# Stick-breaking attention in a decoder layer: the subtraction that makes log beta moved from VectorE to GpSimd

## The chip, the cores and the metric

The kernel runs on one core of a Trainium2 chip. The core has five engines that work side by side: TensorE (PE in the profile; its weight loads are PEld), VectorE (DVE), ScalarE (ACT), GpSimd (POOL) and SyncE (SP), which issues most DMAs. Each engine takes its instructions strictly from its own queue; semaphores order them against the other engines. The metric is the device time of one execution in microseconds.

## The reference

One inference step of a decoder layer, for a prompt of 1024 tokens and 8 sample sequences of 8 tokens with 512 cached ones. The layer is a SwiGLU half step, a mixer (attention, a state-space branch, two gates) and a second SwiGLU half step. What matters here is the attention:

```
z = einsum('bqhd,bkhd->bhqk', q, k) * 64 ** -0.5 + bias
mask = k_pos[None, :] < q_pos[:, None]
log_beta = log_sigmoid(z)
log_keep = where(mask, log_beta - z, 0.0)
after = cumsum(log_keep, axis=3, reverse=True) - log_keep
w = where(mask, exp(log_beta + after), 0.0)
out = einsum('bhqk,bkhd->bqhd', w, v)
```

With e = log(1 + exp(z)), log_beta is z - e and log_keep is -e. A weight is therefore exp(z - e - sum of e over the later keys).

## The kernel before

All matrix products are made in parts: an f32 operand is split into an f16 high part and an f16 rest, so a product takes several f16 matmuls. The stages follow each other: first SwiGLU, the mixer's projections and state-space branch (`mixer_a`, first half), the attention stage (`mixer_a`, second half), the branches' sum (`mixer_b`), second SwiGLU.

In the attention stage `attend_prompt` goes over 4 pairs of heads, 2 chunks of 512 queries and blocks of 128 keys, from the last key block of a chunk down to the first: 4 blocks in the first chunk and 8 in the second, 48 in all. The blocks on the diagonal have 128, 256, 384 and 512 queries, all others 512. A block holds both heads of the pair side by side, so a full block is 128 partitions by 1024 columns; the profile names the smaller ones 256, 512 and 768.

`weights_of` makes one block. TensorE writes the logits into PSUM (L1091, mask L1096); ScalarE makes |z| into tile `ae` (L1098), and z is made into tile `az`, one head by ScalarE (L1100) and one by VectorE (L1102). ScalarE does the exponential and the logarithm in `ae` (L1016, L1017), VectorE adds max(z, 0) (L1018): `ae` now holds e. L1019 makes z - e in place in `az`. ScalarE rounds e, scaled, to f16 (L1021, tile `ah`: the high part), and VectorE makes the rest (L1025), which it writes as f16 into the very tile `ae` from which it reads e:

Of the kernel before, what the change touches and what calls it, by code (L numbers as in the profile page):

```python
# [1004 lines left out]
def weights_of(k, n, hh, rk, acc, logits, after, w=None, first=True, c=(1.0, -1.0)):  # L1005

    nc = k.nc
    v = nc.vector  # L1010
    az = k.ring.tile([P, 2, 512], F32, tag="r", bufs=6, name="az")
    ae = k.ring.tile([P, 2, 512], F32, tag="r", bufs=6, name="ae")
    ah = k.ring.tile([P, 2, 512], F16, tag="h", bufs=4, name="ah")
    z, e = az[:rk, :hh, :n], ae[:rk, :hh, :n]
    logits(az, ae)
    nc.scalar.activation(e, e, AF.Exp, scale=-1.0)  # L1016
    nc.scalar.activation(e, e, AF.Ln, bias=1.0)  # L1017
    v.scalar_tensor_tensor(e, z, 0.0, e, op0=ALU.max, op1=ALU.add)  # L1018
    v.tensor_sub(z, z, e)  # L1019
    hi = ah[:rk, :hh, :n]  # L1020
    nc.scalar.activation(hi, e, AF.Copy, scale=c[0])  # L1021
    if hh == 1:
        after(e)
    lo = ae.bitcast(F16).rearrange("p h (n two) -> p h two n", two=2)[:rk, :hh, 0, :n]
    v.scalar_tensor_tensor(lo, e, c[0], hi, op0=ALU.mult, op1=ALU.subtract)  # L1025
    for h in range(hh):
        for j, part in enumerate((hi, lo)):
            nc.tensor.matmul(acc[:rk, h, :], k.tri[:rk, :rk], part[:, h, :], start=first and j == 0, stop=True,
                             skip_group_check=True)
    v.scalar_tensor_tensor(z, acc[:rk], c[1], z, op0=ALU.mult, op1=ALU.add)  # L1030
    w = z if w is None else w[:rk].unsqueeze(1)
    nc.scalar.activation(w, z, AF.Exp)
    if hh == 2 and after:
        after(hi, lo)
    return w
# [37 lines left out]
def attend_prompt(k, qT, kT, vt, pairs, scales):  # L1073

    nc = k.nc
    for p in pairs:
        qs, ks, inv, c = scales[p]
        for qc in range(2):
# [3 lines left out]
            for j in range(top, -1, -1):  # L1082
# [21 lines left out]
                def rest(hi, lo):  # L1104
                    for h in range(2):
                        for part in (hi, lo):
                            nc.tensor.matmul(acc[:, h, q0:], k.earlier, part[:, h, :], start=False, stop=True,
                                             skip_group_check=True)

                w = weights_of(k, n, 2, P, acc[:, :, q0:], logits, rest if j else None, None, j == top, c)  # L1110
                for h in range(2):
                    nc.tensor.matmul(po[64 * h:64 * h + 64, q0:], vt[:, j, (2 * p + h) * DH:(2 * p + h + 1) * DH],  # L1112
# [11 lines left out]
def attend_sample(k, dr, qT, kT, vt):  # L1124
# [56 lines left out]
    kps = pages("cache_k", NPG - 1)  # L1181
    acc = k.psz.tile([P, 1, 512], F32, tag="z")
    weights_of(k, 512, 1, NS, acc, new_logits, keep_sum(NS, True), w)
    wh = heads(w)
    po = z_tile([P, NB, H // 2, 2, LS])
# [7 lines left out]
    for pg in range(NPG - 1, -1, -1):  # L1193
# [15 lines left out]
        acc = k.psz.tile([P, 1, 512], F32, tag="z")  # L1209
        nc.tensor.matmul(acc[:, 0, :], k.ones, e_sum[:, 0, :], start=True, stop=True, skip_group_check=True)  # L1210
        weights_of(k, 512, 1, P, acc, logits, keep_sum(P, False), w, False)
        vps = pages("cache_v", pg)
        yield
# [628 lines left out]
```

TensorE multiplies both parts with the triangle `tri` (L1028) into the accumulator `P` in PSUM, which gives the sum over the later keys of the block; VectorE combines it with z - e (L1030), ScalarE takes the exponential (L1032), TensorE multiplies with v (L1112). The matmuls with `earlier` (L1107) complete the accumulator for the next block once L1030 has read it. The accumulator has one buffer, the logits' PSUM tiles two, `az` and `ae` share six buffers, `ah` has four.

Three other things share the stage. `attend_sample` attends for the sample tokens, a step after each fourth block: it fetches cache pages by indirect DMAs on GpSimd's queue (L1144, 64 of them in groups of eight; a group takes the four tiles of the group before), multiplies with them (L1155), and uses `weights_of` with hh == 1, five times. The gate projections (`project`, matmuls of L226 with 364 or 360 columns) are placed between the blocks as filler for TensorE until they run out. Their weights are loaded, measured (VectorE's L89 for the maximum of a partition, GpSimd's PARTITION_ALL_REDUCE at L82 across partitions) and split (L101, L102). `scaled_pair` reduces the maxima of the next pair's q and k the same way (GpSimd at L1048).

The order on each engine isn't the order of the code: a scheduler sets it when the program is built, from its own estimate of durations. So an instruction that moves to another engine can change the order on all of them.

## Time and profile before

| | us |
|---|---|
| median of 3 runs | 2384.77 |
| lowest, highest run | 2381.21, 2393.02 |
| the profiled execution's own time | 2397.24 |
| its span, first to last instruction | 2395.5 |
| granted TensorE clock, mean share | 0.982 |

The attention stage reaches from about 1118 to 1490 us of the span. The profile comes from one execution. The page gives the busy time of each engine over the whole span; views by stretch give it for parts. A row of the view in order of time has a start, a duration, the engine, the line, the operation and, in brackets, the idle time of the engine before it and what ended it; "issue" there means that no semaphore of the profile ended it.

### The profile page before, as it was taken

To read this page: it belongs to the slowest core of one execution; us is meant where nothing else is said; L and a number is where in the kernel's file an instruction comes from. 1 tells how busy PE (TensorE), PEld (TensorE's weight loads), DVE (VectorE), ACT (ScalarE), POOL (GpSimd) and SP (SyncE) were. 2 spreads that over 40 slices of the span, in tenths; PEclk is the share of its full clock that TensorE was granted. 3 is DMA by queue.
4 is the path that set the end of the run, shared out by engine and by line. 5 is a ranking of instruction groups with operands and counts; after the bars stand their busy time and mean duration, and the time that the engine had idled before them with its cause. 6 is when DMAs were issued, how large, how long until landed. Compare 5 with 4: busy or idle time off the path is not lost.

```text
span 2395.5 us, 42875 instructions
## 1 busy us (share of the span) xinstructions
PE 2287.6 (95%) x18391; PEld 1626.9 (68%) x18391; DVE 1678.2 (70%) x3026; ACT 969.2 (40%) x1244; POOL 141.8 (6%) x193
## 2 busy tenths in 40 slices
PE   5999999999999999899999997999999999999997
PEld 2677778777787666685544452655688878888884
DVE  5966698886797626446788787697677655777735
ACT  3533331233331521245788787324443321333403
POOL 0000000000000000001133300000000000000000
PEclk8999999999999999989999998999999999999999
DMA  8133334433333144445244323522111143111302
GB/s 308 55 119 108 108 120 140 152 108 123 135 145 126 54 146 146 110 158 185 75 137 136 109 67 128 187 77 84 61 52 55 34 139 111 63 54 54 129 19 76
DMA packets 94191, 262.83 MB, mean 110 GB/s; under 512 B 13152, under 2 KB 50400, under 8 KB 83760
## 3 DMA queue, kind: packets, MB, share of 16 engines
q1 hardware_dynamic: 83632, 240.23, 29.3%
q0 software_dynamic: 5312, 17.34, 2.5%
q10 hardware_dynamic: 5056, 2.52, 0.5%
q8 instruction: 144, 2.36, 0.4%
q14 instruction: 47, 0.39, 0.1%
HBM read 204.10 MB, written 49.66 MB: 106 GB/s over the span
## 4 chain that ended last, share of the span: by engine, by line
PE 54%; DVE 13%; ACT 7%; DMA 5%; issue 3%; POOL 1%; SPq 1%; another core or an unknown queue 0%; ACTq 0%; DVEq 0%; POOLq 0%
PE u L481 19%; PE u L242 13%; PE u L226 11%; PE u L216 2%; PE z L1368 2%; DVE wl L102 2%; DVE mx L89 2%; DMA wf<-in_ffn_w_in 2%; ACT ae L1098 1%; DMA wf<-in_w_in 1%; PE z L226 1%; PE z L994 1%; PE o L1112 1%; DMA aw<-in_ada_w 1%; ACT ae L1016 1%
## 5 line engine op out<-in xcount | busy, mean ns | idle before, releaser
L226 PE MATMUL u<-u,wh 128*128 128x364 f16 (+1 forms) x1632 | 391.6, 319 | 6.3 <-ACT u L398 4.3
L242 PE MATMUL u<-h,wh 128*128 128x272 f16 (+1 forms) x2304 | 366.2, 280 | 4.9 <-DVE h L102 4.9
L101 ACT ACTIVATE wh<-wf,sc 128x1024 f16<-128x1024 f32 (+2 forms) x130 | 183.2, 1410 | 371.4 <-PE u L242 179.8
L89 DVE TENSOR_REDUCE mx<-wf 128x1 f32<-128x1024 f32 (+2 forms) x136 | 211.1, 1575 | 145.3 <-DMA wf<-in_ffn_w_in 80.3
L481 PE MATMUL u<-u,wh 128*128 128x272 f16 (+1 forms) x1824 | 288.0, 279 | 1.7 <-DVE mx L89 1.3
L242 PEld LDWEIGHTS <-wh 128*128 128x128 f16 x2560 | 249.2, 97 | 59.3 <-issue 6.9
L481 PEld LDWEIGHTS <-wh 128*128 128x128 f16 x2432 | 234.6, 98 | 66.3 <-issue 19.7
L226 PE MATMUL u<-u,wl 128*128 128x364 f16 (+1 forms) x816 | 260.2, 319 | 1.1 <-DVE wl L102 1.1
L102 DVE SCALAR_TENSOR_TENSOR wl<-wf,sc,wh 128x1024 f16<-128x1024 f32 (+2 forms) x130 | 209.2, 1609 | 73.3 <-ACT wh L101 72.8
L226 PEld LDWEIGHTS <-wh 128*128 128x128 f16 x1824 | 176.4, 98 | 114.7 <-issue 15.0
L242 PE MATMUL u<-h,wl 128*128 128x274 f16 (+1 forms) x1152 | 228.3, 280 | 0.0
L481 PEld LDWEIGHTS <-w3h 128*128 128x128 f16 x1824 | 175.7, 97 | 43.6 <-issue 7.4
L481 PE MATMUL u<-fac,w3h 128*128 128x272 f16 x1216 | 192.7, 279 | 0.0
L481 PE MATMUL u<-u,wl 128*128 128x272 f16 (+1 forms) x912 | 179.7, 278 | 0.0
L82 POOL PARTITION_ALL_REDUCE am<-mx x106 | 53.8, 514 | 1871.3 <-DVE mx L89 1834.1
L242 PEld LDWEIGHTS <-wl 128*128 128x128 f16 x1280 | 124.3, 97 | 26.9
L481 PEld LDWEIGHTS <-wl 128*128 128x128 f16 x1216 | 118.1, 97 | 26.2 <-issue 0.4
L226 PEld LDWEIGHTS <-wl 128*128 128x128 f16 x912 | 89.3, 98 | 58.3 <-issue 4.6
L481 PE MATMUL u<-fac,w3l 128*128 128x272 f16 x608 | 120.1, 279 | 0.0
L226 PEld LDWEIGHTS <-aside 128*128 128x128 f16 x864 | 83.0, 97 | 50.5 <-issue 1.7
L507 ACT ACTIVATE h<-h,iv 128x546 f32<-128x546 f32 x38 | 28.5, 749 | 206.8 <-DVE h L506 206.8
L481 PE MATMUL u<-fac,wh 128*128 128x272 f16 x608 | 97.9, 284 | 4.0 <-DVE st L523 4.0
(431 smaller groups left out, 3857.7 us busy)
## 6 DMA issues: line engine op xcount, KB each, us to landing
wf<-in_ffn_w_in SPq DMA_DIRECT2D x44, 1024.0 KB
aw<-in_ada_w SPq DMA_DIRECT2D x72, 512.0 KB
wf<-in_w_in SPq DMA_DIRECT2D x16, 1024.0 KB
wf<-in_ffn_w_out_a SPq DMA_DIRECT2D x16, 640.0 KB
xd<-xr SPq DMA_DIRECT2D x16, 546.0 KB
x<-xd SPq DMA_DIRECT2D x16, 546.0 KB
xd<-x SPq DMA_DIRECT2D x6, 1456.0 KB
sg<-gd SPq DMA_DIRECT2D x16, 546.0 KB
```

Source lines behind the costliest of these rows:

```text
L82: k.nc.gpsimd.partition_all_reduce(r, m, P, ABSMAX)
L89: k.nc.vector.tensor_reduce(m, src, axis=axis, op=ALU.max, apply_absolute_value=True)
L101: r = k.nc.scalar.activation(hi, src, AF.Copy, scale=s)
L102: k.nc.vector.scalar_tensor_tensor(lo, src, s, hi, op0=ALU.mult, op1=ALU.subtract)
L216: k.nc.tensor.matmul(ps[:, c, :n], wt[:, cols], act(kt, part)[:, c * CH:c * CH + n], start=kt == 0 and j == 0, stop=kt == nk - 1 and j == 2)
L226: k.nc.tensor.matmul(ps[:, :n], wt[:, cols], act(kt, part)[:, c * CH:c * CH + n], start=kt == 0 and j == 0, stop=kt == nk - 1 and j == 2)
L242: k.nc.tensor.matmul(ps[:, a:b], wt[:, cols], act(kt, part)[:, a0 + a:a0 + b], start=kt == 0 and j == 0, stop=kt == nk - 1 and j == 2)
L481: nc.tensor.matmul(t[:, c0:c1], wt[:, kt * P:kt * P + P], act(kt, part)[:, c0 - 240:c1 - 240], start=first and kt == 0 and j == 0, stop=kt ...
L507: nc.scalar.activation(h2, h2, AF.Silu, scale=iv)
L994: nc.tensor.matmul(p[:, q, :], ca[rows, ri, ga, 1:, :].rearrange("p a b -> p (a b)"), x[rows, ga, :], start=False, stop=ri == 1)
L1016: nc.scalar.activation(e, e, AF.Exp, scale=-1.0)
L1368: nc.tensor.matmul(ps[:M, :256], u[:, kt, part, tt * P:tt * P + M], wt, start=kt == 0 and j == 0, stop=kt == KD - 1 and j == 2)
```

## The change

For the prompt's blocks (hh == 2) L1019 is issued to GpSimd; for the sample's (hh == 1) it stays on VectorE.

```
-    v.tensor_sub(z, z, e)
+    (v if hh == 1 else nc.gpsimd).tensor_sub(z, z, e)
```

The built program differs more than the diff. On GpSimd, near the start of the attention stage, stood before (`pg` are the cache pages, `am` and `sq` maxima over the partitions, shown as ISA):

```order
L82 ISA am<-mx 128x1
L1144 DMA pg<-in_cache_k,rows 128x512 x8
L82 ISA am<-mx_12291 128x1
L1048 ISA sq<-sq 128x2
L1144 DMA pg<-in_cache_v,rows 128x512 x8
L82 ISA am<-mx_12937 128x1
```

and now, from the third subtraction of the first head pair on:

```order
L1019 TENSOR_TENSOR az<-az,ae 128x2x384
L1144 DMA pg<-in_cache_k,rows 128x512
L82 ISA
L82 ISA am<-mx_12291 128x1
L1019 ISA
L1019 TENSOR_TENSOR az<-az,ae 128x1024
L1048 ISA
L1048 ISA sq<-sq 128x2
L1019 ISA
L1019 TENSOR_TENSOR az<-az,ae 128x2x128
L1019 TENSOR_TENSOR az<-az,ae 128x2x256
L1019 TENSOR_TENSOR az<-az,ae 128x2x384
```

Besides the subtractions, a bare row (a line, ISA, no tile) has come ahead of each change between a reduction and a subtraction.

On VectorE the first two blocks of the stage (128 and 256 queries) stood so before:

```order
L1018 SCALAR_TENSOR_TENSOR ae<-az,ae 128x2x128
L1019 TENSOR_TENSOR az<-az,ae 128x2x128
L1025 SCALAR_TENSOR_TENSOR ae<-ae,csqk,ah 128x2x128
L1030 SCALAR_TENSOR_TENSOR az<-P,csqk,az 128x2x128
L102 SCALAR_TENSOR_TENSOR wl<-wf,sc,wh 128x2048
L1102 TENSOR_SCALAR az<-z,csqk,bias 128x256
L1018 SCALAR_TENSOR_TENSOR ae<-az,ae 128x2x256
L1102 TENSOR_SCALAR az<-z,csqk,bias 128x384
L1019 TENSOR_TENSOR az<-az,ae 128x2x256
L1025 SCALAR_TENSOR_TENSOR ae<-ae,csqk,ah 128x2x256
```

and stand so now:

```order
L1018 SCALAR_TENSOR_TENSOR ae<-az,ae 128x2x128
L102 SCALAR_TENSOR_TENSOR wl<-wf,sc,wh 128x2048
L1102 TENSOR_SCALAR az<-z,csqk,bias 128x256
L1018 SCALAR_TENSOR_TENSOR ae<-az,ae 128x2x256
L1102 TENSOR_SCALAR az<-z,csqk,bias 128x384
L1025 SCALAR_TENSOR_TENSOR ae<-ae,csqk,ah 128x2x128
L1025 SCALAR_TENSOR_TENSOR ae<-ae,csqk,ah 128x2x256
L1030 SCALAR_TENSOR_TENSOR az<-P,csqk,az 128x2x128
L1018 SCALAR_TENSOR_TENSOR ae<-az,ae 128x2x384
L1030 SCALAR_TENSOR_TENSOR az<-P,csqk,az 128x2x256
```

The two L1019 rows are gone, and L1025 of the first block has moved behind L1018 of the second and behind other work.

## Rows read from the trace of the kernel before

**Rows 1.** The page's first part: busy us, share of the span, instructions.

```profile
PE 2287.6 (95%) x18391; PEld 1626.9 (68%) x18391; DVE 1678.2 (70%) x3026; ACT 969.2 (40%) x1244; POOL 141.8 (6%) x193
```

**Rows 2.** Busy time by stretch: us, then each engine's busy us (instructions), clock, DMA.

```profile
1118.00:1436.00 318.00, 301.62 (x2162) 158.68 (x2161) 254.66 (x343) 253.48 (x382) 84.47 (x75) 0.98 0.38 116
1436.00:1476.00 40.00, 27.71 (x113) 9.24 (x112) 35.70 (x39) 39.29 (x51) 0.54 (x1) 0.91 0.33 121
```

**Rows 3.** Groups by line, 1118 to 1500: busy us, mean ns | idle before, releasers.

```profile
L1019 DVE TENSOR_TENSOR az<-az,ae 128x1024 f32<-128x1024 f32 x24 | 29.3, 1221 | 0.3
...
L1021 ACT ACTIVATE ah<-ae,csqk 128x1024 f16<-128x1024 f32 x24 | 27.7, 1152 | 0.5 <-DVE ae L1018 0.3
```

**Rows 4.** Waits, 1118 to 1500: who waited for whom, us in total, times, longest.

```profile
POOL pg L1144 <- PE z L1155: 108.3, 10, 21.6
POOL am L82 <- DVE mx L89: 95.0, 7, 50.7
```

**Rows 5.** Groups on GpSimd, whole span: the larger selects.

```profile
L1270 POOL TENSOR_SCALAR_AFFINE_SELECT mask_s<-mask_s 64x512 bf16<-64x512 bf16 x1 | 1.1, 1107 | 1.8 <-DVE mask_s L1269 1.8
```

**Rows 6.** GpSimd in order of time, the kernel's start.

```profile
0.79 0.20 POOL masks.py:197 MEMSET ident<- 128x128 f32 x1 [0.29 <-POOLq L1834]
8.26 0.28 POOL masks.py:199 TENSOR_SCALAR_AFFINE_SELECT ident<-ident 128x128 f32<-128x128 f32 x1 [7.26 <-issue]
32.81 0.41 POOL L82 PARTITION_ALL_REDUCE am<-mx  x1 [24.27 <-DVE mx L89]
```

**Rows 7.** Groups on GpSimd, 1118 to 1490: the page fetches.

```profile
L1144 POOL DMA_INDIRECT pg<-in_cache_k,rows x32 | 43.9, 1371 | 71.8 <-PE z L1155 56.0 <-DVE ob L102 7.9 <-issue 7.6
L1144 POOL DMA_INDIRECT pg<-in_cache_v,rows x32 | 34.8, 1087 | 61.7 <-PE z L1155 52.3 <-issue 7.5 <-remote 1.5
```

**Rows 8.** VectorE in order of time: the first block, subtractions around four places, the last one.

```profile
1125.29 0.43 DVE L1018 SCALAR_TENSOR_TENSOR ae<-az,ae 128x256 f32<-128x256 f32 x1
1125.75 0.42 DVE L1019 TENSOR_TENSOR az<-az,ae 128x256 f32<-128x256 f32 x1
...
1140.94 0.95 DVE L1019 TENSOR_TENSOR az<-az,ae 128x768 f32<-128x768 f32 x1
...
1144.06 1.21 DVE L1019 TENSOR_TENSOR az<-az,ae 128x1024 f32<-128x1024 f32 x1
...
1173.40 1.23 DVE L1019 TENSOR_TENSOR az<-az,ae 128x1024 f32<-128x1024 f32 x1
...
1197.70 1.23 DVE L1019 TENSOR_TENSOR az<-az,ae 128x1024 f32<-128x1024 f32 x1
...
1324.26 0.69 DVE L1019 TENSOR_TENSOR az<-az,ae 128x512 f32<-128x512 f32 x1
...
1329.04 0.96 DVE L1019 TENSOR_TENSOR az<-az,ae 128x768 f32<-128x768 f32 x1
...
1381.28 1.23 DVE L1019 TENSOR_TENSOR az<-az,ae 128x1024 f32<-128x1024 f32 x1
...
1388.77 1.22 DVE L1019 TENSOR_TENSOR az<-az,ae 128x1024 f32<-128x1024 f32 x1
...
1473.78 1.22 DVE L1019 TENSOR_TENSOR az<-az,ae 128x1024 f32<-128x1024 f32 x1
```

**Rows 9.** GpSimd in order of time, the stage's end.

```profile
1485.54 0.35 POOL L82 PARTITION_ALL_REDUCE am<-mx  x1 [14.24 <-DVE mx L89]
```

**Rows 10.** TensorE in order of time: filler matmuls of L226, no wait between them.

```profile
1110.59 0.47 PE L226 MATMUL u<-u,wh 128*128 128x364 f16 x2
...
1110.90 0.32 PE L226 MATMUL u<-u,wl 128*128 128x364 f16 x1
...
1111.06 0.47 PE L226 MATMUL u<-u,wh 128*128 128x364 f16 x2
```

## Prediction

> **What bounds the kernel now.** I read the page's first part, then the busy time by stretch, then the groups of instructions, the waits and the instructions in order of time of the attention stage alone, because the edited line runs nowhere else. The page shows TensorE busy 95% of the span, VectorE 70%, GpSimd 6% [rows 1]. That average hides two stretches. From 1118 to 1436 us TensorE is busy 302 of 318 us, VectorE 255, ScalarE 253: gate projections and sample attention fill the gaps of the prompt's blocks, and TensorE is the bound. From 1436 to 1476 us, the last head pair, the fillers are gone: ScalarE is busy 39.3 of 40 us, VectorE 35.7, TensorE 27.7 [rows 2].
>
> The edited subtraction costs 1221 ns on VectorE for a full block of 1024 columns [rows 3]. Two facts of its place decide the case. First, its input e is overwritten by the next VectorE step: the low part of L1025 is written into e's own tile, so L1025 can't start before the subtraction has read e, and the matmuls with `tri`, the running sum and the weights all stand behind L1025. Before, the subtraction ran beside ScalarE's rounding to the high part (1152 ns against 1221) and added next to nothing to the chain [rows 3]. Second, GpSimd looks free, but its queue runs in order and holds the page fetches, which waited 108 us on TensorE, and the reductions of maxima, which waited 95 us on VectorE [rows 4].
>
> **The change part by part.** *What VectorE loses.* 48 subtractions, 36,864 columns in all, at 1221 ns per 1024: about 44 us [rows 3]. I credit nothing for it. In the first stretch the bound is TensorE, in the second ScalarE [rows 2], and VectorE keeps waiting at L1025 for the same subtraction.
>
> *What GpSimd gains.* No row of before has a two-input operation on GpSimd. The nearest is a one-input select: 1107 ns for 512 columns, or 2.2 us for 1024 [rows 5]. Below it lies VectorE's own 1.22 us, above it twice the select, 4.4 us. I take 2.2 us, the same engine's row: 36 full blocks, 80 us.
>
> *The reloads.* This is the largest term and the diff does not show it. In the built order GpSimd's bare rows (a line, ISA, no tile) mark a change of the code that the engine runs. Before had four of them, none in the attention stage; the changed kernel has twenty more, from one ahead of the first subtraction to one behind the last: nine pairs round a reduction, and two single ones. What one costs shows once in the trace: after the memset ends at 0.99 us, the first select starts at 8.26 us, 7.26 us idle with no semaphore that ended it [rows 6]. The other reload near it is hidden by a wait on VectorE (24.27 us idle), so it shows only an upper bound; the lower bound is nothing, since one cold reload need not repeat [rows 6]. I take 7.26 us: 20 of them are 145 us, and a pair round a 0.4 us reduction [rows 6] is about 15 us in which no subtraction runs.
> The Trainium skill, GPSIMD Engine Reference, section 2.1 "Instruction dispatch", says that the first call into freshly loaded code pays about 6 us (5.95 measured), with nothing visible in the profile. The row here is longer; by the page's figure the exposed sum below would be about 70 us instead of 91, and the forecast some 10 us lower.
>
> *What of it is exposed.* For each place I take GpSimd's work from one subtraction to the next (the first subtraction, the page fetches in between, the pair) and subtract the time that lay between the same two subtractions before. A fetch is 1.47 us of queue: 43.9 + 34.8 us busy and 7.6 + 7.5 us of issue over 64 [rows 7]. At the first single reload L1018 ends at 1125.72 and the subtraction started at 1125.75 [rows 8]; the reload stands behind four page fetches that end at about that time, so the subtraction is about 7.1 us late. The first pair stands between the subtractions of 1140.94 and 1144.06 [rows 8]: 1.7 + 1.5 + 15.0 us in a gap of 3.1, so 15.1 exposed. The widest gap, 1173.40 to 1197.70 [rows 8], has 24.3 us for 2.2 + 7.4 + 15.0: hidden. At 1324.26 to 1329.04 [rows 8] it is 1.1 + 15.0 in 4.8: 11.3. The last pair, 1381.28 to 1388.77 [rows 8], exposes 9.7. Nine gaps of this kind make 88 us, the work in them 172 (17.7 of subtractions, 13 fetches at 1.47, nine pairs): 84 exposed, 91 with the first. The last reload, behind the last subtraction, which ended at 1475.00, has 10.5 us until the maximum of the outputs is reduced at 1485.54 [rows 8, 9]: hidden.
>
> *What is regained.* If all the rest ran at the old pace, 91 us would be added. It can't all be: during an outage TensorE does filler matmuls, which it then need not do later, and ScalarE and VectorE can prepare further blocks (six tiles of the ring tag, three blocks). The built order does this: in the second query chunk of the first pair, 40 filler matmuls in one run, and 54 in all, now stand between the first `tri` matmul of a block and the ones that need L1025; before, two stood there. At 0.155 us each (three in 0.47 us) [rows 10] that is 8.4 us of a 15 us outage. So about half of the 91 is regained; the other half is lost because TensorE had only 16 us idle in the whole stretch [rows 2], and a filler used in an outage is missing where it covered a block's own latency. I take 45 us; the ends are 0 (all regained) and 91.
>
> *The tail.* In the last head pair ScalarE sets the pace [rows 2], and no reload stands there. VectorE is rid of 11 us, but where L1025 stands right behind L1018 in its queue, it now waits 2.2 us and a semaphore instead of working 1.2: up to 1.2 us at each of six of the last eight blocks, 7 us if ScalarE's work covers none of it, 0 if all. I take 4.
> The Trainium skill, SBUF — State Buffer, "Who interferes with whom", adds that a VectorE instruction with two SBUF inputs blocks while GpSimd reads SBUF; L1018 and L1025 are of that kind. No row of before shows it; by that rule the tail would pay its full 7 us, 3 more than I take.
>
> **Sum.** 45 + 4 = 49 us on the profiled execution's 2397.2 us: 2446 us. That execution is 12.5 us above the median of the runs, 2384.8; on the median's scale the forecast is 2434 us, 2% slower. What a measurement of this kernel can tell from no change is about 0.5%, or 12 us.
>
> **The rivals.**
> *Nothing is regained.* The order assumes shorter outages than the chip takes, TensorE stands at the `tri` matmuls in its queue, and page fetches that now stand behind subtractions come late for the sample attention. Price: 91 us, 7 in the tail, and the 1.0 us by which 2.2 exceeds 1.22 on the 18 blocks whose L1025 stands right behind its L1018: about 116 us, 2501. For it: GpSimd's demand in the stage becomes 94 (fetches) + 145 + 80 + 5 = 324 us, in a queue that must keep order with TensorE, in a stretch of 358 us. At 4.4 us a subtraction the demand is 404 and this case is certain. Against it: the order visibly moved fillers into the outages.
>
> *Everything is hidden.* The fillers cover the outages and the wide gaps take in the rest: 0 to 12 us, 2385 to 2397. For it: the demand of 324 us still fits the stretch. Against it: six pairs stand in gaps under 9 us.
>
> *Faster.* If a reload in the stage took under about 2 us, a pair would fit the gap of 4.8 us behind its 1.1 us of subtraction; VectorE's 44 us would then be a real relief. TensorE could gain at most its 16 us idle [rows 2], so about 13: 2372. For it: only one reload, at the kernel's start, shows a price. Against it: nothing in that row looks disturbed.
>
> **How the numbers follow.** The forecast (20 to 85 us more): 0.62. Nothing regained (85 to 125 more): 0.16; worse than that: 0.04. Hidden: 0.12. Faster: 0.06. The likeliest is the forecast, 2434 us. The range 2397 to 2510 leaves out the hidden and the faster case and the worst one, about 2 in 10. Faster by over 0.5%: 0.06; within: 0.12; slower: 0.82.
>
> **What would show it.** Right: bare idle times of GpSimd near 7 us ahead of reductions and subtractions, with no releaser; TensorE's waits at `tri` (L1028) for L1025 grown from a few us to tens; L1025 released by GpSimd's L1019; the stage's end shifted by 30 to 80 us, and nothing moved after it. GpSimd subtractions near 2.2 us at 1024 columns. The tail as long as before within 7 us. Wrong: reloads of 1 to 2 us; or subtractions over 4 us, in which case their price and not the reloads' is the cause; or a change of time outside the attention stage.

## The result and the profile after

The changed kernel takes 2479.84 us (median of 4 runs, 2474.69 to 2485.10) against 2386.89 us of the kernel before on the same chip: ratio 1.0383, interval 1.0367 to 1.0399, so 93 us slower. The forecast was 49 us. The two profiled executions, 2477.8 and 2395.5 us of span, are 82 us apart: the one before took 2397.24 us, 10 us above the median of its kernel.

The page's first part of the changed kernel (busy us, share of the span, instructions) answers to [rows 1]:

```profile
PE 2315.2 (93%) x18391; PEld 1635.0 (66%) x18391; DVE 1652.9 (67%) x2978; ACT 975.7 (39%) x1244; POOL 236.0 (10%) x241
```

The number of matmuls is the same, yet TensorE is busy 28 us longer; VectorE is rid of 25 us, not of 44. The stage as a whole, from 1118 us to the first output matmul behind it, in the view by stretch; the line of before, then that of after:

```profile
1118.00:1483.80 365.80, 332.47 (x2282) 168.51 (x2280) 294.21 (x383) 293.82 (x433) 85.00 (x76) 0.97 0.38 118
```

```profile
1118.00:1564.10 446.10, 356.65 (x2280) 176.41 (x2278) 268.56 (x334) 299.61 (x433) 178.94 (x124) 0.90 0.31 97
```

The stage is 80.3 us longer. TensorE stands idle 89 of 446 us instead of 33 of 366, which is 56 us; the other 24 us are the same matmuls at a lower granted clock, 0.90 instead of 0.97.

Where the time goes is seen in ScalarE's weight exponentials (L1032) in order of time: the first block, the last block of the second head pair, and the last of the fourth. Before, and then after:

```profile
1129.23 0.42 ACT L1032 ACTIVATE az<-az 128x256 f32<-128x256 f32 x1 [1.08 <-DVE az L1030]
...
1311.69 1.06 ACT L1032 ACTIVATE az<-az 128x1024 f32<-128x1024 f32 x1 [1.60 <-issue]
...
1480.80 1.06 ACT L1032 ACTIVATE az<-az 128x1024 f32<-128x1024 f32 x1 [5.51 <-DVE az L1030]
```

```profile
1136.37 0.41 ACT L1032 ACTIVATE az<-az 128x256 f32<-128x256 f32 x1
...
1373.06 1.05 ACT L1032 ACTIVATE az<-az 128x1024 f32<-128x1024 f32 x1
...
1561.09 1.06 ACT L1032 ACTIVATE az<-az 128x1024 f32<-128x1024 f32 x1 [5.59 <-DVE az L1030]
```

The shift is 7.1 us at the first block, 61.4 at the end of the second pair, 80.3 at the end. It grows through the stage and stays as it is behind it (80.3 at the stage's end, 82.3 at the end of the span).

GpSimd in order of time around the first pair of reloads:

```profile
1139.00 1.83 POOL L1019 TENSOR_TENSOR az<-az,ae 128x768 f32<-128x768 f32 x1
1140.98 1.78 POOL L1144 DMA_INDIRECT pg<-in_cache_k,rows  x1 [0.16 <-issue]
1149.06 0.41 POOL L82 PARTITION_ALL_REDUCE am<-mx  x1 [6.30 <-issue]
1156.79 2.33 POOL L1019 TENSOR_TENSOR az<-az,ae 128x1024 f32<-128x1024 f32 x1 [7.32 <-issue]
1165.09 0.66 POOL L1048 PARTITION_ALL_REDUCE sq<-sq  x1 [5.96 <-DVE az L1030]
1172.86 5.93 POOL L1019 TENSOR_TENSOR az<-az,ae 128x256 f32<-128x256 f32 x3 [7.11 <-issue]
```

Two subtractions that started 3.1 us apart [rows 8] now start 17.8 us apart, with 6.30 and 7.32 us of idle time round a reduction of 0.41 us. The reload at the kernel's start [rows 6] does repeat, in either direction: the nine ahead of a reduction show 5.75 to 7.00 us of idle time, the ten ahead of a subtraction 6.91 to 7.71, nine of the nineteen with nothing that ended them. Where a step is named behind such a time, as at 1165.09, it need not be what GpSimd waited for: the maxima that this reduction reads were done at 1161.40 (VectorE's L89). The twentieth reload stands behind the last subtraction and is hidden (see the tail below).

The waits of the stage in the changed kernel (1118 to 1575 us; us in total, times, longest); the groups of the subtraction and of the low part behind it follow:

```profile
POOL az L1019 <- DVE ae L1018: 93.5, 20, 15.4
...
DVE ae L1025 <- POOL az L1019: 69.7, 28, 6.0
ACT az L1032 <- DVE az L1030: 61.7, 25, 7.6
PE P L1028 <- DVE ae L1025: 55.4, 24, 5.5
```

Before (1118 to 1500 us), TensorE's wait at the triangle was:

```profile
PE P L1028 <- DVE ae L1025: 7.8, 9, 2.2
```

The two groups after, and the low part's before:

```profile
L1019 POOL TENSOR_TENSOR az<-az,ae 128x1024 f32<-128x1024 f32 x24 | 56.3, 2350 | 94.8 <-DVE ae L1018 50.6 <-issue 14.5 <-PE z L1155 14.4
```

```profile
L1025 DVE SCALAR_TENSOR_TENSOR ae<-ae,csqk,ah 128x1024 f16<-128x1024 f32 x24 | 37.4, 1566 | 44.7 <-POOL az L1019 44.7
...
L1025 DVE SCALAR_TENSOR_TENSOR ae<-ae,csqk,ah 128x256 f16<-128x256 f32 x8 | 8.0, 1002 | 14.8 <-POOL az L1019 13.5 <-ACT ah L1021 1.3
```

```profile
L1025 DVE SCALAR_TENSOR_TENSOR ae<-ae,csqk,ah 128x1024 f16<-128x1024 f32 x24 | 33.8, 1410 | 3.1 <-ACT ah L1021 2.5
...
L1025 DVE SCALAR_TENSOR_TENSOR ae<-ae,csqk,ah 128x256 f16<-128x256 f32 x8 | 4.0, 505 | 1.1 <-ACT ah L1021 0.9
```

The chain is to be read upward from the matmul: TensorE waits 55 us at the triangle for L1025 (8 before; the difference is most of the 56 us by which its idle time grew), L1025 waits 70 us for GpSimd's subtraction, and that is a subtraction of 2.35 us (VectorE's took 1221 ns [rows 3]) which starts late. Not all of it are reloads: the 70 us are 28 waits, and there are twenty reloads, ten of them ahead of a reduction.

### The profile page after: what moved, and what is told of

Read it like the earlier page. It is cut to its first block, busy times and chain, and to the rows that moved or that the text cites. A ratio compares the mean times of both kernels' runs of the same rounds, so it can differ in the third digit from the quotient of the medians.

```text
span 2477.8 us, 43002 instructions
## 1 busy us (share of the span) xinstructions
PE 2315.2 (93%) x18391; PEld 1635.0 (66%) x18391; DVE 1652.9 (67%) x2978; ACT 975.7 (39%) x1244; POOL 236.0 (10%) x241
## 4 chain that ended last, share of the span: by engine, by line
PE 66%; DVE 16%; DMA 6%; issue 4%; ACT 4%; POOL 4%; SPq 1%; ACTq 0%; DVEq 0%; POOLq 0%
PE u L481 26%; PE u L242 15%; PE u L226 12%; PE u L216 3%; POOL az L1019 2%; PE z L1368 2%; DVE mx L89 2%; DMA wf<-in_ffn_w_in 2%; DVE wl L102 2%; DVE ae L1025 1%; DMA aw<-in_ada_w 1%; POOL pg L1144 1%; PE s L292 1%; PE P L1028 1%; DVE ae L1018 1%
## 5 line engine op out<-in xcount | busy, mean ns | idle before, releaser
L226 PE MATMUL u<-u,wh 128*128 128x364 f16 (+1 forms) x1632 | 400.0, 326 | 8.0 <-ACT u L398 4.1
L89 DVE TENSOR_REDUCE mx<-wf 128x1 f32<-128x1024 f32 (+2 forms) x136 | 211.0, 1575 | 135.9 <-DMA wf<-in_ffn_w_in 78.7
L226 PE MATMUL u<-u,wl 128*128 128x364 f16 (+1 forms) x816 | 265.2, 325 | 1.1 <-DVE wl L102 1.1
L226 PEld LDWEIGHTS <-wh 128*128 128x128 f16 x1824 | 180.0, 99 | 122.5 <-issue 22.4
L226 PEld LDWEIGHTS <-wl 128*128 128x128 f16 x912 | 90.5, 99 | 61.3 <-issue 8.0
L226 PEld LDWEIGHTS <-aside 128*128 128x128 f16 x864 | 82.9, 97 | 51.8 <-issue 1.7
L1025 DVE SCALAR_TENSOR_TENSOR ae<-ae,csqk,ah 128x1024 f16<-128x1024 f32 (+3 forms) x48 | 65.3, 1374 | 72.3 <-POOL az L1019 69.7
```

The lines of the kernel that those rows point to most:

```text
L89: k.nc.vector.tensor_reduce(m, src, axis=axis, op=ALU.max, apply_absolute_value=True)
L226: k.nc.tensor.matmul(ps[:, :n], wt[:, cols], act(kt, part)[:, c * CH:c * CH + n], start=kt == 0 and j == 0, stop=kt == nk - 1 and j == 2)
```

## The experiments

Each time below is compared with the kernel before on the same chip. A difference from the kernel before is known to about 0.3%, 7 us; where two such differences are set against each other, to some 8 us. The lines of a kernel are its own: where a row names another line than before, the text ahead says which step it is.

### Without the reloads: e1_no_reload and its control e7_ref_max

In the attention stage the maxima over the partitions are made by TensorE and VectorE (transposes, a reduction along the row, a matmul with ones that spreads the result), so GpSimd runs no reductions there. e1 does this to the changed kernel, e7 to the kernel before.

```
-    nc.gpsimd.partition_all_reduce(r, m, P, ABSMAX)
+    if getattr(k, "pe_max", False):
+        tensor_max(k, r, m)
+    else:
+        nc.gpsimd.partition_all_reduce(r, m, P, ABSMAX)
```

> The subtraction stays on GpSimd as in the changed kernel, but the maxima over the partitions that the attention stage needs are made by TensorE (transpose, VectorE maximum, matmul with ones), so GpSimd changes its code once into the stage and once out of it instead of twenty times. Theory (reloads in front of the subtractions hold L1025): most of the 93 us goes, 2390 to 2415 us, with GpSimd's subtraction still 2.35 us for 1024 columns. Rival 1 (the slower subtraction itself, 2.35 us in place of 1.22 on 48 blocks, and VectorE and GpSimd blocking each other): 2445 to 2475. Rival 2 (page fetches and reductions come late behind the reloads): also gone, 2390 to 2415.

> Control: the kernel before with the stage's maxima made by TensorE as in e1_no_reload, the subtraction on VectorE. Every theory: within 12 us of the kernel before (2375 to 2399); what it differs by is to be taken off e1_no_reload.

Measured: e1 2441.68 us, ratio 1.0226 (1.0203 to 1.0248), 54 us over before; e7 2410.12 us, ratio 1.0100 (1.0076 to 1.0124), 22 us over before. Both came out above what the theory gave; e1 lies just below the range of rival 1, the slower subtraction itself. The other way to the maxima comes with 22 us by itself. In the profiled executions e7's stage, from the first logits matmul to the first output matmul behind it, is only 6 us longer than that of before (380.3 against 374.8 us), so where the other 16 us are lost is not shown. What the subtraction on GpSimd adds to the control, with two reloads left of twenty, is 32 us, which the theory had not foreseen. The waits of e1 (L1034 is the subtraction, L1040 the low part, L1043 the triangle):

```profile
DVE ae L1040 <- POOL az L1034: 59.6, 29, 6.3
...
PE P L1043 <- DVE ae L1040: 34.5, 23, 6.4
```

The low part waits for the subtraction about as often and nearly as long as with the reloads. If the control's 22 us add up with the rest, which no run separates, the reloads in the changed kernel are worth 93 - 32 = 61 us (with the same control by the stage, 47; see the sum of the runs).

### The reloads without the subtraction: e2_tiny_on_chain, e3_tiny_off_chain, e11_tiny_no_reload

The subtraction stays on VectorE. GpSimd gets one of four columns in each block, whose result nobody reads: it makes the reloads, and next to no work. In e2 it reads e, so that L1025, which overwrites e, must wait for it; in e3 it reads the high part, and nothing of the block waits for it but the buffer. e11 is e2 with the maxima by TensorE, thus with two reloads, to be set against e7.

```
+    if hh == 2:
+        t = k.ring.tile([P, 2, 2], F32, tag="tiny", bufs=2, name="tiny")
+        nc.gpsimd.tensor_sub(t, e[:, :, :2], e[:, :, 2:4])
```

> The kernel before, with the whole subtraction on VectorE, plus a GpSimd subtraction of 4 columns per prompt block that reads e (its result is not used), so GpSimd reloads as often as in the changed kernel and L1025 has to wait for it, but the operation itself is nearly free. Theory: the reloads alone do it, 2440 to 2480 us. Rival 1 (price of the long subtraction): 2387 to 2410. Rival 2 (late fetches and reductions): 2440 to 2480.

> As e2_tiny_on_chain, but the 4-column GpSimd subtraction reads the high part (tile ah) instead of e, so the reloads and the order of the queue stay and nothing on a block's chain waits for them: only page fetches, reductions and, four blocks later, the tile's reuse. Theory: 2385 to 2405 us. Rival 1: 2385 to 2395. Rival 2 (late fetches and reductions): 2430 to 2480.

> The control e7 (maxima of the stage by TensorE) with the four-column subtraction of e2 on GpSimd, which L1025 must wait for: the handing over to GpSimd and back in each of the 48 blocks, without reloads between (one in, one out) and without the length of the real subtraction. Theory (the 42 us of e2 are its twenty reloads): within 8 us of e7, 2403 to 2418 us. Rival (they are the hand-over of each block): 2430 to 2450 us. It also splits the 32 us between e1 and e7: what e11 lacks to e1 is the length of the real subtraction.

Measured: e2 2429.78 us, 1.0174 (1.0149 to 1.0200), 42 us over before; e3 2412.55 us, 1.0102 (1.0078 to 1.0126), 25 us; e11 2416.22 us, 1.0126 (1.0101 to 1.0150), 30 us over before and so 8 over its control.

e2 stays below the 2440 us that the theory "the reloads alone do it" needed. Handing the blocks over to GpSimd and back costs 8 us in all, which these times alone can hardly tell from nothing; the reloads on the chain are therefore some 34 of e2's 42. The rest of e1's 32 us, 24, goes with the real subtraction, which takes 2.44 us there for a full block. What its reads do to VectorE is not much of it: the low part, which waits for it, then takes 1398 ns in e1 and 1407 in the control. The waits of e2 (L1024 the small subtraction, L1028 the low part), then of e11 (L1039 and L1043):

```profile
POOL tiny L1024 <- issue: 42.3, 6, 7.5
...
DVE ae L1028 <- POOL tiny L1024: 24.7, 13, 5.0
```

```profile
DVE ae L1043 <- POOL tiny L1039: 11.6, 7, 3.3
```

e3 cost more than the theory allowed, although no block waits in it, and less than the 2430 us at which the range of late fetches and reductions began. The waits show where: the reductions themselves come 6 us late, and VectorE, which needs the maximum for the scale, waits for them; before, that wait (`sc` for `am`) was 0.7 us. First the row of before, then those of e3 (L1051 is L1048, L1052 is L1049):

```profile
DVE sc L74 <- POOL am L82: 0.7, 2, 0.5
```

```profile
DVE sc L74 <- POOL am L82: 12.2, 6, 6.4
POOL am L82 <- issue: 12.2, 2, 6.5
POOL sq L1051 <- issue: 12.2, 2, 6.2
DVE sq L1052 <- POOL sq L1051: 9.1, 2, 5.7
```

So a reload hurts on both of its sides: the reduction ahead of which it stands has readers too. That these waits make up the 25 us is not shown; the profiled stage of e3 is only 9 us longer than that of before (383.7 against 374.8 us).

### The wait at L1025: e4_own_low, e6_own_low_no_reload, e10_before_own_low

The low part gets a tile of its own, so that L1025 no longer overwrites what the subtraction reads. Only L1030 still needs the subtraction's result, two steps later.

```
-    lo = ae.bitcast(F16).rearrange("p h (n two) -> p h two n", two=2)[:rk, :hh, 0, :n]
+    if hh == 1:
+        lo = ae.bitcast(F16).rearrange("p h (n two) -> p h two n", two=2)[:rk, :hh, 0, :n]
+    else:
+        al = k.ring.tile([P, 2, 512], F16, tag="l", bufs=2, name="al")
+        lo = al[:rk, :hh, :n]
```

e4 is the changed kernel with it, e6 is e1 with it, e10 the kernel before with it and nothing else.

> The changed kernel, but the low part of L1025 goes into a tile of its own (f16, 2 buffers) in place of the bytes of e, so that L1025 has no more reason to wait for GpSimd's read of e; reloads of GpSimd's code and the price of the subtraction stay, and only the exponent at L1030 still needs its result. Theory (the chain runs sub -> L1025 -> triangular matmuls, where 69.7 us of VectorE's waits stand): most of what lies on the chain comes back, 2405 to 2440 us, and the wait of L1025 for GpSimd is gone. Rival (the chain runs over the result of the subtraction, so it is only handed on from L1025 to L1030; or GpSimd's reads slow VectorE): 2455 to 2485 us, with the 69.7 us standing at L1030.

> e1 (no reductions on GpSimd in the stage, subtraction on GpSimd) with the low part in a tile of its own as in e4. e1 stood at 2441.7 us and its control e7, with the subtraction on VectorE, at 2410.1. Theory (the 32 us between them are VectorE waiting at L1025 for the subtraction): 2405 to 2420 us. Rival (they come from VectorE's own operations being slower beside GpSimd, or from the result coming late to L1030): 2430 to 2445 us.

> Control for e4, e6 and e9: the kernel before with the low part in a tile of its own and nothing else. Theory (the extra tile by itself costs and gives nothing, so what e4 gave back is the wait at L1025): 2380 to 2396 us, within 0.4% of before. Rival (the own tile is itself a gain, by the earlier release of buffers): under 2378 us.

Measured: e4 2436.42 us, 1.0198 (1.0172 to 1.0224), 47 us over before; e6 2418.57 us, 1.0123 (1.0101 to 1.0144), 29 us over before and 7 over the control e7; e10 2394.98 against 2396.60 us, 0.9996 (0.9983 to 1.0008): the tile by itself gives nothing.

So half of the 93 us hangs on the one overwrite, and without reloads e6 gets back all but 7 of e1's 32 us. In e4 the wait at the low part (L1029 there) for GpSimd is gone, and part of it has moved to L1034, which is L1030:

```profile
DVE az L1034 <- POOL az L1019: 34.6, 11, 7.2
ACT az L1036 <- DVE az L1034: 33.5, 18, 5.0
```

Eleven waits of up to 7.2 us, the length of a reload, where the matmuls of the triangle have run meanwhile. In e6, without reloads, fewer and shorter ones are left (L1049 is L1030 there, L1034 the subtraction):

```profile
DVE az L1049 <- POOL az L1034: 14.7, 5, 4.8
```

### Is there anything to gain on VectorE: e9_sub_behind_low

The kernel before with the low part's own tile, and the subtraction, still on VectorE, written behind L1025: the 1.22 us are off the way to the triangle, and GpSimd has nothing to do with it.

```
-    v.tensor_sub(z, z, e)
+    if hh == 1:
+        v.tensor_sub(z, z, e)
...
     v.scalar_tensor_tensor(lo, e, c[0], hi, op0=ALU.mult, op1=ALU.subtract)
+    if hh == 2:
+        v.tensor_sub(z, z, e)
```

> The kernel before, everything on VectorE, but the low part in a tile of its own as in e4, and the subtraction of the blocks with two heads written behind L1025, so that the low part and its triangular matmuls no longer stand behind it. Theory (what the changed kernel could have gained without GpSimd is 1.22 us a block on the way to the matmuls, and before, VectorE's waits around it were short, so little of it is on the path): 2368 to 2390 us, same or slightly faster than before. Rival (VectorE's order is what sets the stage, so the whole 24 x 1.22 us and more comes back): under 2360 us. Rival (the subtraction is now what L1030 waits behind): 2392 to 2410 us.

Measured: 2401.11 against 2396.60 us, 1.0017 (1.0007 to 1.0027), 0.2% slower; the theory's 2368 to 2390 us is missed. Moved off the way to the triangle, the subtraction brings nothing. VectorE still does it here, ahead of L1030, so this run does not show what it would be worth to free VectorE of the 44 us altogether. No version here beats the kernel before.

### GpSimd's reads beside VectorE: e8_load_off_chain

The control e7 with a full-width subtraction of the high part from itself on GpSimd, whose result nobody reads. GpSimd is busy with it for as long as in e1 (89 us), but no block waits for it.

```
+        t = k.ring.tile([P, 2, 512], F32, tag="idle", bufs=1, name="idle")
+        nc.gpsimd.tensor_sub(t[:, :, :n], hi, hi)
```

> The control e7 (subtraction on VectorE, maxima of the stage by TensorE) with a full-width subtraction on GpSimd beside it, of the high part from itself into a tile that nobody reads: GpSimd has as much to do as in e1, and nothing waits for it but the buffer of the high part. Theory (the 32 us between e1 and e7 are dependencies): 2405 to 2418 us. Rival (they are VectorE being held up by GpSimd's accesses): 2425 to 2445 us, with longer durations at the two VectorE operations that follow.

Measured: 2429.18 us, 1.0170 (1.0149 to 1.0191), 40 us over before and so 18 over the control; of the expectation, this is the rival's range. The groups of the low part (L1040 in the control, L1043 in e8), of the control and then of e8:

```profile
L1040 DVE SCALAR_TENSOR_TENSOR ae<-ae,csqk,ah 128x1024 f16<-128x1024 f32 x24 | 33.7, 1407 | 1.4 <-ACT ah L1036 0.9
```

```profile
L1043 DVE SCALAR_TENSOR_TENSOR ae<-ae,csqk,ah 128x1024 f16<-128x1024 f32 x24 | 53.5, 2235 | 1.4 <-ACT ah L1036 0.9
...
L1048 DVE SCALAR_TENSOR_TENSOR az<-P,csqk,az 128x1024 f32<-128x1024 f32 x24 | 30.8, 1282 | 6.0 <-PE P L1046 5.6
```

The low part reads e and the high part, both in SBUF, and takes 828 ns more on average; L1048 (L1030) has one of its inputs in PSUM and takes 1282 ns, as in the kernel before (1283), also in the four blocks in which it ran beside GpSimd's subtraction (1284). One block of the slow kind in order of time, GpSimd, then VectorE, and VectorE in a block with no GpSimd beside it:

```profile
1216.45 1.89 POOL L1039 TENSOR_TENSOR idle<-ah 128x1024 f32<-128x1024 f16 x1 [8.70 <-ACT ah L1036]
```

```profile
1216.72 2.83 DVE L1043 SCALAR_TENSOR_TENSOR ae<-ae,csqk,ah 128x1024 f16<-128x1024 f32 x1
...
1230.96 1.39 DVE L1043 SCALAR_TENSOR_TENSOR ae<-ae,csqk,ah 128x1024 f16<-128x1024 f32 x1
```

VectorE starts 0.27 us behind GpSimd and needs 2.83 us: the 1.62 us for which GpSimd still runs, and 1.21. It does nearly all of its own work after GpSimd has ended. The other order occurs too. Here VectorE starts 0.10 us ahead; it takes its usual 1.39 us, and GpSimd 3.00 instead of 1.89:

```profile
1480.13 1.39 DVE L1043 SCALAR_TENSOR_TENSOR ae<-ae,csqk,ah 128x1024 f16<-128x1024 f32 x1 [0.87 <-ACT ah L1036]
...
1480.23 3.00 POOL L1039 TENSOR_TENSOR idle<-ah 128x1024 f32<-128x1024 f16 x1 [4.29 <-ACT ah L1036]
```

The Trainium skill, SBUF — State Buffer, "Who interferes with whom", says this: a VectorE instruction with two SBUF inputs contends with a GpSimd instruction that reads SBUF, and who issues first has the shared ports while the other blocks. Both pairs of rows agree (2.83 against 1.39 us for VectorE, 3.00 against 1.89 for GpSimd). Not every block of e8 fits by its start times: at 1223.66 us VectorE starts 0.23 us ahead and yet takes 3.35 us.

In the changed kernel this price is smaller, because L1025 waits for its own block's subtraction anyway and meets only that of another block: by the groups after and before, 1566 against 1410 ns in the 24 full blocks and 1002 against 505 in the eight smallest, 3.7 + 4.0 us of VectorE; with the sixteen blocks in between it is 13 us. That is most of why VectorE is rid of 25 us and not of 44. Where the wait is taken away, the price comes back in part: in e6 the low parts take 60.9 us in all, in the control 53.0. Whether these 8 us are e6's last 7, or the 14.7 us of waits at L1030, wasn't separated.

### One head pair alone: e5_last_pair

GpSimd makes the subtraction in the last of the four head pairs only, with four reloads: the expectation counted two, but the trace has a reduction in the middle of the pair, with a reload on either side.

```
-    (v if hh == 1 else nc.gpsimd).tensor_sub(z, z, e)
+    (nc.gpsimd if k.on_pool and hh == 2 else v).tensor_sub(z, z, e)
...
+        k.on_pool = p == 3
```

> GpSimd makes the subtraction in the last head pair alone, which has two reloads (the first subtraction after the pair's reductions, and the next user of GpSimd behind the stage) where the changed kernel has twenty, and all of the tail. Theory (the price goes by the reloads on the chain and the waits for the subtraction, so by the number of pairs): a quarter of 93 us less the pair boundaries that are left out, 2395 to 2415 us. Rival (the tail, where TensorE has no other work, carries most of it): over 2425 us. Rival (the cost lies at the boundaries between pairs alone): 2387 to 2395 us.

Measured: 2403.51 us against 2389.21, ratio 1.0073 (1.0047 to 1.0098), 14 us by the medians and 17 by the ratio: a sixth of the 93. The number of reloads (four of twenty) would give 19 and the number of pairs (one of four) 23; the interval, 11 to 23 us, doesn't decide between them. The tail doesn't carry most of the cost. The run's waits, eight in the pair's twelve blocks:

```profile
POOL az L1019 <- DVE ae L1018: 72.8, 9, 37.0
...
DVE ae L1025 <- POOL az L1019: 17.2, 8, 4.9
```

### The sum of the runs

The first column of times goes by the medians. The second goes by the stage in the profiled executions, one of each kernel, from the first logits matmul to the first output matmul behind the stage: 374.8 us before, 380.3 in e7, 390.1 in e11, 406.3 in e2, 413.9 in e1, 415.7 in e4 and 455.4 in the changed kernel.

| what | from | us, medians | us, stage |
|---|---|---|---|
| handing over to GpSimd and back | e11 - e7 | 8 | 10 |
| the real subtraction and GpSimd's reads, without reloads | e1 - e11 | 24 | 24 |
| the reloads, with a subtraction of no length | e2 less the handing over | 34 | 22 |
| what is left when both come together | changed kernel less these | 27 | 25 |
| changed kernel over before | | 93 | 81 |
| of it, behind the overwrite of e | changed kernel - e4 | 46 | 40 |

The first three lines of medians are good to some 8 to 10 us and the fourth to some 11; they assume that the control's extra time adds up with the rest. The two columns differ where a run is set against the kernel before: all kernels with a changed stage but e9 and e10 lose 6 to 17 us more against its median than their stage shows, and where these are lost is not shown. So the reloads alone are worth 22 to 34 us, and together with the real subtraction (the third line and the fourth) 47 to 61.

The fourth line is not explained by a run of its own. GpSimd's queue is fuller there: 179 us busy in the stage and some 130 of reloads, of 446 us, where e2 has 110 and 130 of 391. Yet it was not full, since the subtraction waited 93.5 us for VectorE's L1018. That a late reload then falls on a late subtraction is argued, not shown, and so is what a rival would have it be: the order of the built program on all engines, which each of these edits can change.

## Why the prediction was right in sign and half in size

**What bounds, and the worth of VectorE's 44 us: not contradicted.** They were credited with nothing. e9 bears on this in part: the subtraction off the way to the triangle gives 1.0017. That VectorE would gain nothing by being free of the 44 us is argued from [rows 2], and no run shows it.

**The overwrite of e as the point that decides: right for half.** e4 takes it away and 46 us come back (40 by the stage), and e10 shows that this is not the tile.

**The reloads, their number and price: right.** Twenty of them, 5.75 to 7.71 us each where they show, against 7.26 taken [rows 6]. The first block came 7.1 us later, as worked out; the first pair with its reduction took 14.0 us, against 15.0 taken. The rule of the Trainium skill, GPSIMD Engine Reference, "Instruction dispatch", of about 6 us in the first call into freshly loaded code, agrees with most of those ahead of a reduction (5.75 to 6.30 us in eight of nine); those ahead of a subtraction, 6.91 to 7.71, are longer.

**Half of the 91 us regained: right in the main for the reloads.** 45 us were forecast as left of them. Alone, by e2, they cost 22 to 34, and with the real subtraction beside them 47 to 61.

**The sum left out the subtraction's own length: this is the step that failed.** The prediction took 2.2 us for a full block, 2.35 was measured (89 us of GpSimd for all 48 blocks, where 80 were taken), against 1.22 on VectorE, and it put a price on that in the tail only (4 us). In the first stretch the sum has the subtraction only inside the gaps round a pair of reloads. That VectorE "keeps waiting at L1025 for the same subtraction" was said there, but only to credit nothing for VectorE's relief, and a longer wait at the 48 blocks was left at nothing. The longer wait was priced in a rival alone (1.0 us on 18 blocks, and 7 in the tail: 25 us). e1 - e11 shows 24 us and the handing over 8, with two reloads left of twenty. The reason is in the rows of after: 28 waits of L1025, on a chain that TensorE follows.

**And the two do not merely add up.** Another 27 us (25 by the stage) appear when long subtractions and reloads come together; the cause of this part stays open. The rival "Nothing is regained" (116 us) put it down to a queue that is too full to keep order with TensorE, and the result of 93 lies nearer to it than to the forecast of 49. But its reason is not borne out as it stands, by GpSimd's 93.5 us of waiting for L1018.

**That fillers give back what an outage takes: only at full clock.** The prediction reckoned with 0.155 us for a filler matmul [rows 10]. TensorE around the first pair of reloads, in order of time and by stretch:

```profile
1148.75 0.32 PE L226 MATMUL u<-u,wh 128*128 128x364 f16 x1
1151.41 0.58 PE L1028 MATMUL z<-ah,tri 64*64 64x512 f16 x1 [2.35 <-ACT ah L1021]
1151.93 0.48 PE L226 MATMUL u<-u,wh 128*128 128x364 f16 x1
1152.21 0.51 PE L226 MATMUL u<-u,wl 128*128 128x364 f16 x1
1152.51 0.81 PE L226 MATMUL u<-u,wh 128*128 128x364 f16 x2
```

```profile
1149.00:1151.40 2.40, 0.07 (x1) 0.10 (x1) 1.79 (x7) 0.63 (x1) 0.41 (x1) 0.96 0.21 73
1151.40:1157.50 6.10, 6.09 (x18) 2.20 (x17) 1.76 (x4) 1.06 (x2) 0.71 (x1) 0.50 0.00 0
```

TensorE stood idle for 2.35 us, and in the 6.1 us after that it is granted 0.50, the 1.2 GHz level: the fillers start 0.30 us apart, not 0.155. The outage is filled, but at half the work. Over the stage a matmul takes 156.4 ns on average against 145.7 (356.65 us over 2280, 332.47 over 2282): 24 of the stage's 80 us. The same reckoning gives some 10 us for e2 (339.41 us over 2262) and 13 for e1 over its control (349.57 over 2308, 337.33 over 2313).

**The tail: right.** 4 us were taken, between bounds of 0 and 7. From the first to the last subtraction of the last chunk, before on VectorE 1436.52 to 1473.78 us, 37.3; after on GpSimd:

```profile
1512.63 0.72 POOL L1019 TENSOR_TENSOR az<-az,ae 128x256 f32<-128x256 f32 x1 [15.39 <-DVE ae L1018]
...
1554.46 2.35 POOL L1019 TENSOR_TENSOR az<-az,ae 128x1024 f32<-128x1024 f32 x1 [5.94 <-DVE ae L1018]
1565.87 0.41 POOL L82 PARTITION_ALL_REDUCE am<-mx  x1 [9.06 <-DVE mx L89]
```

41.8 us, 4.5 more and not the full 7. The last row answers to [rows 9]: the reload behind the last subtraction lies inside the 9.06 us in which GpSimd waits for VectorE, so it is hidden, as worked out.

## What to carry to other kernels

Before an operation goes to an idle engine, look for who overwrites its input: here the next step wrote into the operand, so the engine that was meant to be rid of the work waited for it, and a tile of its own took back half of the loss. Look in the built program for the rows of code changes on GpSimd: here an operation between reductions cost two reloads a time, and the reductions' readers paid as well as its own. And an outage that is filled with other work is not free: TensorE's granted clock was 0.50 just then.

## What the runs showed of the hardware

- Each change on GpSimd between the reduction over partitions and a two-input operation shows as idle time, 5.75 to 7.00 us ahead of the reduction and 6.91 to 7.71 ahead of the subtraction; going back to what ran shortly before costs no less (nineteen times in the stage).
- Its subtraction of f32 takes 2350 ns for 128 x 1024, 1.9 times VectorE's, and 728 for 128 x 256.
- Of a VectorE instruction with both inputs in SBUF and a GpSimd subtraction, the one that started later did its work after the other (VectorE 2.83 us instead of 1.39 when it started 0.27 us later, GpSimd 3.00 instead of 1.89 when it started 0.10 us later). VectorE's L1030, which reads one input from PSUM, took 1284 ns beside such a subtraction and 1281 alone.
- After one idle time of 2.35 us, TensorE's granted clock was 0.50 in the 6.10 us behind it, while it was busy for 6.09 of them.
